# Even and odd tokens apart in a token tile: dilated attention within a parity, probabilities transposed in place, values in one visit

## The chip, the core and the metric

One core of a Trainium2 chip runs the program. The metric is the device time of one execution in microseconds (us), shown as the median of several runs. TensorE is called PE below (PEld is its weight load), VectorE DVE, ScalarE ACT, and SP is the engine whose queue issues most of the loads.

## The reference, cut to what matters

Three blocks in a row work on 256 tokens of width 1024: a feed-forward block, a mixer (a gated linear recurrence beside sliding-window attention with 16 heads) and a second feed-forward block; then two equal layers, each with a short convolution branch, a latent attention with 8 heads (MLA) and a dilated attention, all gated and summed. Everything is fp32.

The dilated attention has 3 groups of 8 heads of width 64. Group 0 looks back over 128 tokens one by one; group 1 sees every 4th token up to 512 back, group 2 every 16th up to 2048 back. With 256 tokens the last two see every key of their own residue that isn't in the future.

```
DIL_PATTERNS = ((128, 1), (512, 4), (2048, 16))
s = q.k * scale - slope * dilation * j      # j steps back, 0 <= j <= window // dilation
o_g, lse_g = softmax over the keys of group g
o_c = sum over g of softmax(lse)_g * o_g    # one softmax over the keys of all three groups
```

So a query of group 1 or 2 only ever attends to keys whose distance is a multiple of 4 or 16: always an even one.

## The kernel before, in words

Tokens stand in two tiles of 128 (a tile is one set of partitions). Every large product is made in three matmuls, high times high, high times low, low times high (`mm3`, L222 to L226), and its weights are streamed: SP loads a piece into one of 4 buffers `raw`, ACT rounds it to `w` high (L207), DVE subtracts to `w` low (L208), into one of 8 buffers. These streams are the bulk of PE's work: `gu`, `dn` (feed-forward), `g`, `xg` (mixer), `dqk`, `bz`, `gp`, `po`, `cx`, `zb`, `o` (layers).

Attention is threaded into the streams. After every few matmuls a stream calls `tick`, which advances a modelled time and lets one of three lanes issue its next piece: `tp` (transposes of queries and keys), `S` (scores and softmax) and `T` (values). The order in which the pieces are issued is thus set by that modelled time; each engine then works in order.

A layer has four `DilPair`s (m = 0 to 3), each with two heads (j) of all three groups. For each pair:

- `chunk`/`evac` project queries, keys and values (`dqk`); values are copied from PSUM to `vd` by two ACT copies (L1221).
- `scores` (L1248) goes over the three groups. `score_pair` (L787) makes for each head a 128x128 product for the first token tile and a 128x256 one for the second; the head's 64 channels stand in its own 64 partitions. A custom DVE operation adds scaled distances (1e33 where a key is not seen) and takes the maximum (L1260); after the third group ACT takes the exponentials (L1268), DVE sums and scales them (L1269 to L1274).
- `values` (L1277) goes over the groups again: `prob_T` (L771) transposes three 128x128 blocks for each head into a PSUM bank, ACT copies them to a tile `pt` (L776), and `pv_pair` (L779) accumulates values times probabilities in `dyT`, each head in its own 64 output columns. So PE is visited three times for values. `gated` then multiplies by the gate.

The mixer's attention (`attn1`) and MLA use `heads` (L712), which has the same pieces for one group: 8 pairs of heads in the mixer and 4 in each layer; each pair is a score piece, two `prob_T` and a value piece `yT`.

At the start SP loads the first token tile in two halves (`load_x`, L274), then the gain `g`, the first weight piece and the second token tile; at the end `residual` (L1131) adds and stores each tile in two halves.

Of the kernel before, what the change touches and what calls it, by code (L numbers as in the profile page):

```python
# [14 lines left out]
ALU = mybir.AluOpType  # L15
# [12 lines left out]
MIXER_POOLS = (("l2", 13), ("s", 4), ("pt", 4), ("gth", 2), ("c1", 3))  # L28
LAYER_POOLS = (("dil", 9), ("s", 5), ("pt", 4), ("gth", 2), ("c1", 3))
# [18 lines left out]
def host_constants():  # L48

    f = np.float32  # L50
    pos = np.arange(S, dtype=f)

    def rope(half, inv):
        ang = pos[:, None] * inv[None, :]
# [8 lines left out]
    q = np.arange(P)[:, None]  # L63
    k = np.arange(S)[None, :]
    diff = P + q - k
    dist = []
    for window, dil in ((128, 1), (512, 4), (2048, 16)):
        ok = (diff >= 0) & (diff % dil == 0) & (diff // dil <= window // dil)
        dist.append(np.where(ok, diff.astype(f), f(1e33)))
    kk = k[:, :P]  # L70
# [4 lines left out]
    slopes = (f(2.0) ** (f(-8.0) * np.arange(1, 25, dtype=f) / f(24))).astype(f)  # L75
    qs = np.broadcast_to((f(-0.125) / slopes)[None, :], (P, 24))
    pack = np.concatenate([c2, s2] + dist + [mask2, qs, c1, s1, mask1], 1)
    return np.ascontiguousarray(pack.astype(f)), [float(x) for x in slopes]
# [3 lines left out]
CW = CONST.shape[1] - 512  # L82

# [13 lines left out]
class Kern:  # L97
# [176 lines left out]
    def load_x(self, t):  # L274
        for f in range(2):
            c = slice(f * 512, (f + 1) * 512)
            self.nc.sync.dma_start(out=self.h[t][:, c], in_=self.a["x"][0, t * P:(t + 1) * P, c])

    def params(self):
# [13 lines left out]
        self.dist = take(768).rearrange("p (g k) -> p g k", g=3)  # L293
# [275 lines left out]
    def mixer(self, xT):  # L569
# [142 lines left out]
    def heads(self, pairs, v, mask, scale, emit, deps, out, sinks=None):  # L712
# [39 lines left out]
        def values():  # L752
            for m in range(len(pairs)):
                while len(ready) <= m or self.now < ready[m][1]:
                    yield 0.0, 0.3
                s = ready[m][0]
                yp = self.bank("yp", "yT", (P, S))
                pts = []
                for j in range(2):
                    yield from self.room()  # L760
                    pts.append(self.prob_T([s[:, j, b * P:(b + 1) * P] for b in range(3)]))
                    yield 0.32, W_T
                self.live -= 1
                self.pv_pair(yp, v[m], pts, True, True)
                emit(m, yp)
                yield 1.1, 0.0
# [12 lines left out]
    def pv_pair(self, yp, v, pts, first, last):  # L779
        m = self.nc.tensor.matmul  # L780
        for b in range(2):
            c = slice(P * b, S)
            for j in range(2):
                m(yp[64 * j:64 * j + 64, c], lhsT=v[j][b], rhs=pts[j][:, 0:S] if b == 0 else pts[j][:, S:384],
                  start=first and b == 0, stop=last and b == 1)
# [9 lines left out]
    def lru(self, pp, xT, w, out):  # L795
# [19 lines left out]
        for j in range(2):  # L815
            f = f0 + j
            xpad = self.tl("c1", [P, S + 3], "xpad")
            nc.vector.memset(xpad[:, 0:3], 0.0)
            nc.scalar.copy(xpad[:, 3:], banks[j][:, 0])
            xc = self.t([P, S], "xc")  # L820
            nc.scalar.activation(xc, xpad[:, 0:S], AF.Identity, scale=self.conv_w[:, 0, f:f + 1], bias=self.conv_b[:, f:f + 1])
            for k in range(1, 4):
                stt(xc, in0=xpad[:, k:k + S], scalar=self.conv_w[:, k, f:f + 1], in1=xc, op0=ALU.mult, op1=ALU.add)
            xcs.append(xc)
        for j in range(2):
            gb = banks[j][:, 1]
            u = self.t([P, S], "gu2")
            nc.scalar.activation(u, gb, AF.Square)
            stt(u, in0=u, scalar=1.0 / 0.044715, in1=gb, op0=ALU.add, op1=ALU.mult)
            nc.scalar.activation(u, u, AF.Tanh, scale=0.7978845608028654 * 0.044715)  # L830
            stt(GG[:, j], in0=u, scalar=1.0, in1=gb, op0=ALU.add, op1=ALU.mult)
# [269 lines left out]
    def conv_branch(self, l, xT, w):  # L1101
# [5 lines left out]
        for pp in range(2):  # L1107
# [3 lines left out]
            for j in range(2):  # L1111
                f = 2 * pp + j
                upad = self.tl("c1", [P, S + 2], "upad")
                nc.vector.memset(upad[:, 0:2], 0.0)
                tmp = self.t([P, S], "ac")
                nc.scalar.copy(tmp, b1[j][:, 0])
                tt(upad[:, 2:], tmp, b1[j][:, 1], op=ALU.mult)
                nc.scalar.activation(cv[:, j], upad[:, 0:S], AF.Identity, scale=cw[:, 0, f:f + 1], bias=cb[:, f:f + 1])
                for k in range(1, 3):
                    stt(cv[:, j], in0=upad[:, k:k + S], scalar=cw[:, k, f:f + 1], in1=cv[:, j], op0=ALU.mult, op1=ALU.add)  # L1120
            b2 = self.pairB(rows(xT), [col(3), col(0)], "zb")
            for j in range(2):
# [3 lines left out]
                tt(cv[:, j], cv[:, j], b2[j][:, 1], op=ALU.mult)  # L1126
                stt(cv[:, j], in0=cv[:, j], scalar=0.5, in1=sz, op0=ALU.mult, op1=ALU.mult)
                self.split(hi[:, f], lo[:, f], cv[:, j])
        return (hi, lo)

    def residual(self, t, accs, out=None):  # L1131
        nc = self.nc
        for f in range(2):
            c = slice(f * 512, (f + 1) * 512)
            nc.vector.tensor_tensor(self.h[t][:, c], accs[f], self.h[t][:, c], op=ALU.add)
            if out is not None:
                nc.sync.dma_start(out=out[t * P:(t + 1) * P, c], in_=self.h[t][:, c])
# [56 lines left out]
class DilPair:  # L1194
# [21 lines left out]
    def evac(self, which, ts, accs):  # L1216
        k, nc, m = self.k, self.k.nc, self.m
        if which == 2:
            self.dst[2] = k.tl("dil", [P, 2, 384], "vd")
            for t in ts:  # L1220
                nc.scalar.copy(self.dst[2][:, t], accs[t])  # L1221
# [3 lines left out]
        if which == 0 and self.gt is None:  # L1225

            self.gt = k.tl("pt", [P, 6, 64], "gt")
# [13 lines left out]
    def attend(self, sz, yc, out):  # L1241
        k, nc, m = self.k, self.k.nc, self.m
        ready = []
        qd, kd, vd = self.dst[0], self.dst[1], self.dst[2]
        sides = ((0, slice(0, P), slice(P, S)), (1, slice(P, 384), slice(0, S)))
        rows = [slice(64 * j, 64 * j + 64) for j in range(2)]

        def scores():  # L1248
            yield from k.after(*self.jobs)
            mx, nm, rs = (k.small([P, 2, 2], x) for x in ("dmx", "dnm", "drs"))  # L1250
            sm = k.small([P, 2, 2, 3], "dsm")
            ss = []
            for g in range(3):
# [3 lines left out]
                ps = k.score_pair([(qd[r, g], kd[r, g]) for r in rows])  # L1257
                for j in range(2):
                    for t, c, dc in sides:
                        nc.vector.tensor_tensor_reduce(  # L1260
                            s[:, j, c], in0=ps[j][:, c], in1=k.dist[:, g, dc], scale=-SLOPES[8 * g + 2 * m + j],
                            scalar=-3e38 if g == 0 else mx[:, j, t:t + 1], op0=ALU.add, op1=ALU.max, accum_out=mx[:, j, t:t + 1])
                yield 1.1, W_SC
            nc.vector.tensor_scalar(nm, mx, -1.0, None, op0=ALU.mult)
            for g, s in enumerate(ss):
                for j in range(2):
                    for t, c, _ in sides:
                        nc.scalar.activation(s[:, j, c], s[:, j, c], AF.Exp, bias=nm[:, j, t:t + 1], accum_out=sm[:, j, t, g:g + 1])  # L1268
            nc.vector.tensor_reduce(rs, sm, axis=mybir.AxisListType.X, op=ALU.add)  # L1269
            nc.vector.reciprocal(rs, rs)  # L1270
            for s in ss:
                for j in range(2):
                    for t, c, _ in sides:
# [3 lines left out]
        def values():  # L1277
            if not yc:
                yc.extend([k.b4([P, 4, S], "ych", F32R), k.b4([P, 4, S], "ycl", F32R)])
            while not ready or k.now < ready[0][1]:  # L1280
                yield 0.0, 0.3
            yp = k.bank("yp", "dyT", (P, S))
            for g, s in enumerate(ready[0][0]):
                pts = []
                for j in range(2):
                    yield from k.room()
                    pts.append(k.prob_T([s[:, j, b * P:(b + 1) * P] for b in range(3)]))
                    yield 0.32, W_T
                k.live -= 1
                k.pv_pair(yp, [[vd[:, b, (2 * g + j) * 64:(2 * g + j + 1) * 64] for b in range(2)] for j in range(2)], pts, g == 0, g == 2)  # L1290
                yield 1.1, 0.0
            k.gated(yc, sz, m, yp)
            yield 0.64, 0.0
# [36 lines left out]
```

## Time and profile before

| | |
|---|---|
| runs | 1349.64, 1346.84, 1347.28 us, median 1347.28 |
| the profiled execution | 1345.55 us, of which 1343.8 us are the span from first to last instruction |
| PE busy | 1313.7 us (98% of the span), 9434 matmuls |
| PE weight loads busy | 1215.6 us (90%) |
| DVE busy | 948.5 us (71%) |
| ACT busy | 784.5 us (58%) |
| DMA | 230.30 MB, mean 171 GB/s |

Busy times are unions of an engine's instructions. PE's are pipelined: two that follow each other overlap in the listing, so what one costs is read from start to start. A program matmul on fp32 data (scores, values) stands in the trace as two matmul records, each with its own weight load; one of `mm3` stands as one.

### The profile page before, as it was taken

What the parts mean: (1) busy time and instruction counts of PE and PEld (TensorE: products, weight loads), DVE (VectorE), ACT (ScalarE), POOL (GpSimd) and SP (SyncE); (2) the same over time, 40 slices, a digit from 0 to 9 for tenths busy, and PEclk for the clock granted to TensorE, in tenths of its full rate; (3) what the DMA queues carried; (4) which work ended last, traced back from release to release, by engine and by line L of the source; (5) the groups of instructions that cost most, each with busy time, mean ns of one, the idle gap of its engine ahead of it and who ended that gap; (6) DMA issues with size and microseconds to landing.
All of it is one profiled execution on the core that took longest, in us unless ns stands there. A gap on an engine that the chain in (4) does not pass through costs nothing.

```text
span 1343.8 us, 24690 instructions
## 1 busy us (share of the span) xinstructions
PE 1313.7 (98%) x9434; PEld 1215.6 (90%) x9434; DVE 948.5 (71%) x2178; ACT 784.5 (58%) x1468; POOL 3.0 (0%) x10
## 2 busy tenths in 40 slices
PE   6999999999999999999999999999999999999998
PEld 5899988989997899998998889999899988899997
DVE  6547667897868655568888676666788886765663
ACT  6444544788745544455667776554456667755451
POOL 0000000000000000000000000000000000000000
PEclk9999999999999999999999999999999999999999
DMA  7757764445565566673755454666656543546661
GB/s 255 226 166 234 224 219 142 139 146 135 169 213 179 176 197 191 205 231 98 212 142 131 126 173 126 180 186 194 179 157 186 142 128 104 173 145 187 193 195 52
DMA packets 234806, 230.30 MB, mean 171 GB/s; under 512 B 12336, under 2 KB 213184, under 8 KB 234688
## 3 DMA queue, kind: packets, MB, share of 16 engines
q1 hardware_dynamic: 232432, 227.05, 56.8%
q10 hardware_dynamic: 2256, 1.67, 0.5%
q8 instruction: 74, 1.21, 0.4%
q14 instruction: 44, 0.36, 0.1%
HBM read 227.64 MB, written 1.05 MB: 170 GB/s over the span
## 4 chain that ended last, share of the span: by engine, by line
PE 75%; DVE 11%; ACT 6%; DMA 5%; issue 2%; SPq 0%; ACTq 0%; DVEq 0%
PE gu L224 5%; PE gu L226 5%; PE gu L225 5%; PE gp L224 3%; DVE w L208 3%; PE gp L225 3%; PE gp L226 3%; PE dqk L224 3%; PE dqk L226 3%; PE dn L226 3%; PE dn L225 3%; PE dqk L225 3%; PE dn L224 3%; DMA raw<-in_w_in_dram 3%; PE po L224 2%
## 5 line engine op out<-in xcount | busy, mean ns | idle before, releaser
L208 DVE TENSOR_TENSOR w<-raw,w 128x1024 fp32r<-128x1024 f32 (+1 forms) x437 | 501.8, 1156 | 222.3 <-ACT w L207 218.5
L207 ACT CAST w<-raw 128x1024 fp32r<-128x1024 f32 (+1 forms) x437 | 433.3, 999 | 334.4 <-PE gu L226 51.1
L224 PE MATMUL gu<-xh,w 128*128 128x256 f32 x576 | 159.6, 277 | 0.0
L226 PE MATMUL gu<-xh,w 128*128 128x256 f32 x576 | 159.2, 276 | 0.0
L225 PE MATMUL gu<-xl,w 128*128 128x256 f32 x576 | 159.1, 276 | 0.0
L224 PE MATMUL dqk<-w,xh 128*128 128x384 f32 x384 | 136.5, 355 | 0.0
L225 PE MATMUL dqk<-w,xh 128*128 128x384 f32 x384 | 129.5, 337 | 0.0
L226 PE MATMUL dqk<-w,xl 128*128 128x384 f32 x384 | 129.2, 336 | 0.0
L225 PEld LDWEIGHTS gu<-xl,w 128*128 128x128 f32 x576 | 108.2, 188 | 0.6
L224 PEld LDWEIGHTS gu<-xh,w 128*128 128x128 f32 x576 | 108.1, 188 | 0.6
L224 PE MATMUL gp<-xh,w 128*128 128x256 f32 x384 | 108.3, 282 | 0.0
L226 PEld LDWEIGHTS gu<-xh,w 128*128 128x128 f32 x576 | 108.2, 188 | 0.0
L226 PE MATMUL gp<-xh,w 128*128 128x256 f32 x384 | 106.4, 277 | 0.0
L225 PE MATMUL gp<-xl,w 128*128 128x256 f32 x384 | 106.2, 277 | 0.0
L224 PEld LDWEIGHTS dqk<-w,xh 128*128 128x128 f32 x384 | 72.2, 188 | 6.2 <-issue 6.0
L224 PEld LDWEIGHTS gp<-xh,w 128*128 128x128 f32 x384 | 72.1, 188 | 2.7 <-issue 2.7
L225 PEld LDWEIGHTS dqk<-w,xh 128*128 128x128 f32 x384 | 72.4, 189 | 0.2
L226 PEld LDWEIGHTS gp<-xh,w 128*128 128x128 f32 x384 | 72.2, 188 | 0.0
L226 PEld LDWEIGHTS dqk<-w,xl 128*128 128x128 f32 x384 | 72.2, 188 | 0.0
L225 PEld LDWEIGHTS gp<-xl,w 128*128 128x128 f32 x384 | 72.2, 188 | 0.0
L226 PE MATMUL dn<-w,aT 128*128 128x512 f32 x176 | 69.1, 393 | 0.0
L225 PE MATMUL dn<-w,aT 128*128 128x512 f32 x176 | 68.9, 391 | 0.0
(378 smaller groups left out, 3242.6 us busy)
## 6 DMA issues: line engine op xcount, KB each, us to landing
raw<-in_w_in_dram SPq DMA_DIRECT2D x140, 512.0 KB
raw<-in_ffn_w_gu_dram SPq DMA_DIRECT2D x88, 512.0 KB
raw<-in_w_in_dram SPq DMA_DIRECT2D x192, 192.0 KB
raw<-in_ffn_w_down_dram SPq DMA_DIRECT2D x44, 512.0 KB
raw<-in_w_o_dram SPq DMA_DIRECT2D x16, 512.0 KB
raw<-in_w_proj_attn_dram SPq DMA_DIRECT2D x16, 256.0 KB
raw<-in_w_proj_lru_dram SPq DMA_DIRECT2D x8, 512.0 KB
raw<-in_w_out_dram SPq DMA_DIRECT2D x8, 512.0 KB
```

The source lines that it names most:

```text
L207: nc.scalar.copy(hi, raw)
L208: nc.vector.tensor_tensor(lo, raw, hi, op=ALU.subtract)
L224: m(out, lhsT=ah, rhs=bh, start=first, stop=False)
L225: m(out, lhsT=ah, rhs=bl, start=False, stop=False)
L226: self.last = m(out, lhsT=al, rhs=bh, start=False, stop=last).ins
```

## The change

Inside each tile of 128 tokens the order becomes: the 64 even ones, then the 64 odd ones. Loads of x and stores of the output are split by parity (twice as many, half as large), tables of cosines, masks and distances are built in that order, and where the order in time matters (the convolutions and the recurrence) operations that are there anyway read or write through a view that puts the tokens back (`natural`, `by_parity`). One operation of the mixer (L831) becomes two halves.

Groups 1 and 2 then need only products within a parity: `score_parity` makes, for each group, head j and parity e, a 64x128 and a 64x64 product, written for both groups into one pair of PSUM banks as large as those of one group before. Softmax thus goes over two score tiles instead of three. Values for groups 1 and 2 are kept by parity (`vp`), with the first tile's values of both groups above each other, so that one product serves both groups there.

`prob_T` copies the transposed blocks back over the probabilities; the tiles `pt` are gone. In `values` all transposes come first, then all value products in one visit; `heads` takes two pairs of heads together.

```diff
-MIXER_POOLS = (("l2", 13), ("s", 4), ("pt", 4), ("gth", 2), ("c1", 3))
-LAYER_POOLS = (("dil", 9), ("s", 5), ("pt", 4), ("gth", 2), ("c1", 3))
+MIXER_POOLS = (("l2", 13), ("s", 5), ("gth", 2), ("c1", 3))
+LAYER_POOLS = (("dil", 9), ("s", 5), ("v0", 2), ("gt", 2), ("gth", 2), ("c1", 3))
...
+def natural(x):
+    return x.rearrange("p (t i e) -> p t e i", i=64, e=2)
+def by_parity(x):
+    return x.rearrange("p (t e i) -> p t e i", i=64, e=2)
...
     def load_x(self, t):
+        x = self.a["x"][0, t * P:(t + 1) * P].rearrange("(i e) c -> e i c", e=2)
         for f in range(2):
             c = slice(f * 512, (f + 1) * 512)
-            self.nc.sync.dma_start(out=self.h[t][:, c], in_=self.a["x"][0, t * P:(t + 1) * P, c])
+            for e in range(2):
+                self.nc.sync.dma_start(out=self.h[t][64 * e:64 * e + 64, c], in_=x[e, :, c])
...
-                        self.split(yl[c][0][:, q], yl[c][1][:, q], out[2 * c + i])
+                        flat = lambda z: z.rearrange("p f s -> p (f s)")
+                        self.split(by_parity(flat(yl[c][0][:, q])), by_parity(flat(yl[c][1][:, q])), natural(flat(out[2 * c + i])))
...
-    def prob_T(self, parts):
-        ps = self.bank("x", "pT", (P, 384))
-        for b, x in enumerate(parts):
-            self.nc.tensor.transpose(ps[:, b * P:(b + 1) * P], x, self.id)
-        pt = self.tl("pt", [P, 384], "pt")
-        self.nc.scalar.copy(pt, ps)
-        return pt
+    def prob_T(self, s):
+        for j in range(2):
+            yield from self.room()
+            ps = self.bank("x", "pT", (P, 384))
+            for b in range(3):
+                c = slice(b * P, (b + 1) * P)
+                self.nc.tensor.transpose(ps[:, c], s[:, j, c], self.id)
+            self.nc.scalar.copy(s[:, j], ps)
+            yield 0.32, W_T
...
     def evac(self, which, ts, accs):
         if which == 2:
-            self.dst[2] = k.tl("dil", [P, 2, 384], "vd")
-            for t in ts:
-                nc.scalar.copy(self.dst[2][:, t], accs[t])
+            v0, vp = k.tl("v0", [P, 2, P], "v0"), k.tl("dil", [P, 6, P], "vp")
+            self.dst[2] = v0, vp
+            g12 = [acc[:, P:384].rearrange("p (g c) -> p g c", g=2) for acc in accs]
+            for t in range(2):
+                for e in range(2):
+                    nc.scalar.copy(vp[64 * t:64 * t + 64, 2 * e:2 * e + 2], g12[t][64 * e:64 * e + 64])
+                nc.scalar.copy(v0[:, t], accs[t][:, 0:P])
+                if t == 0:
+                    for e in range(2):
+                        for g in range(2):
+                            nc.scalar.copy(vp[64 * g:64 * g + 64, 4 + e], g12[0][64 * e:64 * e + 64, g])
...
+        def score_parity():
+            ps = [k.bank("x", "sc", (P, 384)) for _ in range(2)]
+            for g in range(2):
+                for j, r in enumerate(rows):
+                    for e in range(2):
+                        tok = lambda t: slice(P * t + 64 * e, P * t + 64 * e + 64)
+                        o = ps[j][64 * e:64 * e + 64]
+                        nc.tensor.matmul(o[:, P + g * P:S + g * P], lhsT=qd[r, 1 + g, tok(1)],
+                                         rhs=kd[r, 1 + g].rearrange("p (t e i) -> p e t i", t=2, e=2)[:, e], start=True, stop=True)
...
+                        nc.tensor.matmul(o[:, g * 64:g * 64 + 64], lhsT=qd[r, 1 + g, tok(0)], rhs=kd[r, 1 + g, tok(0)], start=True, stop=True)
...
-            for g in range(3):
+            for i in range(2):
                 s = yield from k.s_tile(2)
...
-                ps = k.score_pair([(qd[r, g], kd[r, g]) for r in rows])
+                ps = score_parity() if i else k.score_pair([(qd[r, 0], kd[r, 0]) for r in rows])
...
+            s0, s1 = ready[0][0]
+            for s in (s0, s1):
+                yield from k.prob_T(s)
             yp = k.bank("yp", "dyT", (P, S))
...
+            k.pv_pair(yp, [[v0[:, b, hd[j]] for b in range(2)] for j in range(2)], s0, True, False)
+            for i, c in ((4, 0), (5, 64), (0, P), (2, P + 64), (1, S), (3, S + 64)):
+                o = c if c < S else c - P
                 for j in range(2):
...
+                    nc.tensor.matmul(yp[hd[j], o:o + 64], lhsT=vp[:, i, hd[j]], rhs=s1[:, j, c:c + 64], start=False, stop=i == 3)
```

How the order on PE moves is seen at the first value piece of a layer's dilated attention, inside the stream `dqk` of the next pair (sc are scores, dyT values, pT transposes of probabilities; a row is line, operation, what it writes and reads, output partitions x columns, how often). Before:

```order
L226 MATMUL dqk<-w,xl 128x384
L784 MATMUL dyT<-pt,vd 64x256 x2
L784 MATMUL dyT<-pt,vd 64x128 x2
L792 MATMUL sc<-qkd 128x128 x2
L792 MATMUL sc<-qkd 128x256 x2
L224 MATMUL dqk<-w,xh 128x384
```

With the change, on the same engine:

```order
L246 MATMUL dqk<-w,xl 128x384
L810 MATMUL dyT<-s,v_7183 64x256 x2
L810 MATMUL dyT<-s,v_7183 64x128 x2
L1352 MATMUL dyT<-s,vp 64x64 x12
L1299 MATMUL sc<-qkd 64x128 x4
L1305 MATMUL sc<-qkd 64x64 x4
L1299 MATMUL sc<-qkd 64x128 x4
L1305 MATMUL sc<-qkd 64x64 x4
L244 MATMUL dqk<-w,xh 128x384
```

What were three value pieces and two of three score pieces, spread over the stream, is now one value piece of 16 matmuls and one score piece of 16, which here follow each other. The copies of the values on ACT, in the first layer, were before:

```order
L207 CAST w<-raw 128x1024 x2
L1221 COPY vd<-dqk 128x384 x2
L207 CAST w<-raw 128x1024
```

and are now:

```order
L1257 COPY vp<-dqk 64x256 x2
L1258 COPY v_7183<-dqk 128x128
L1262 COPY vp<-dqk 64x128 x4
L1257 COPY vp<-dqk 64x256 x2
L1258 COPY v_7183<-dqk 128x128
```

Ten copies stand where two stood, ahead of the roundings of weights that follow on ACT.

## Rows read from the trace of the kernel before

**Rows 1.** The page's part 1: busy us, share, instructions of each engine.

```profile
PE 1313.7 (98%) x9434; PEld 1215.6 (90%) x9434; DVE 948.5 (71%) x2178; ACT 784.5 (58%) x1468; POOL 3.0 (0%) x10
```

**Rows 2.** Busy time by stretch: bounds, length, engines, granted clock, DMA share, GB/s.

```profile
600.00:780.00 180.00, 176.17 (x1123) 163.06 (x1122) 146.50 (x503) 119.38 (x276) 0.00 (x0) 1.00 0.49 133
780.00:970.00 190.00, 189.51 (x1558) 179.15 (x1557) 127.03 (x235) 106.90 (x192) 0.00 (x0) 1.00 0.62 181
```

**Rows 3.** Waits of PE: us in all, how many, the longest.

```profile
PE tp L391 <- DVE hn L380: 9.7, 1, 9.7
...
PE po L224 <- ACT ylh L214: 1.6, 1, 1.6
```

**Rows 4.** Timeline of PE, one value and one score piece: start, duration, instruction.

```profile
796.37 0.28 PE L226 MATMUL gp<-xh,w 128*128 128x256 f32 x1
796.58 0.87 PE L784 MATMUL dyT<-pt,vd 128*64 128x256 f32 x8
797.38 0.93 PE L792 MATMUL sc<-qkd 64*128 64x128 f32 x8
798.24 0.39 PE L224 MATMUL gp<-xh,w 128*128 128x256 f32 x1
798.46 0.28 PE L225 MATMUL gp<-xl,w 128*128 128x256 f32 x1
798.58 0.28 PE L226 MATMUL gp<-xh,w 128*128 128x256 f32 x1
798.69 0.49 PE L774 MATMUL pT<-ident,s 128*128 128x128 f32 x3
...
799.15 0.28 PE L225 MATMUL gp<-xl,w 128*128 128x256 f32 x1
```

**Rows 5.** Groups of PE's instructions by form (count; busy us, mean ns).

```profile
L774 PE MATMUL pT<-ident,s 128*128 128x128 f32 x240 | 39.4, 273 | 1.8 <-DVE mx L728 1.0 <-ACT qkd L1237 0.8
...
L784 PE MATMUL dyT<-pt,vd 128*64 128x256 f32 x96 | 15.7, 405 | 0.0
L792 PE MATMUL sc<-qkd 64*128 64x256 f32 x96 | 14.4, 377 | 0.0
...
L784 PE MATMUL yT<-pt,kv 128*64 128x256 f32 x32 | 5.9, 404 | 0.0
...
L784 PE MATMUL yT<-pt,vm 128*64 128x256 f32 x32 | 5.2, 404 | 0.0
```

**Rows 6.** Timeline of PE at 797.38 us, the window cut after two matmuls.

```profile
797.38 0.38 PE L792 MATMUL sc<-qkd 64*128 64x128 f32 x2
```

**Rows 7.** Chain of waits, a score piece of MLA (96 partitions deep).

```profile
701.97 1.31 PE sc L792 x8
```

**Rows 8.** Chain of waits, 736 to 800 us: start, us, what.

```profile
745.81 3.53 ACT s L1268 x16
...
750.14 2.75 DVE s L1274 x12
...
781.09 4.95 DMA raw<-in_w_in_dram
```

**Rows 9.** Groups of ACT's instructions by form.

```profile
L1268 ACT ACTIVATE s<-s,dnm 128x256 f32<-128x256 f32 x48 | 24.0, 500 | 0.0
...
L1221 ACT COPY vd<-dqk 128x384 f32<-128x384 f32 x16 | 7.2, 492 | 1.1 <-PE dqk L226 1.1
...
L214 ACT CAST ylh<-lGG 128x512 fp32r<-128x512 f32 x4 | 2.4, 624 | 2.8 <-DVE lGG L866 2.8
```

**Rows 10.** Timeline of the first 20 us: SP, DVE and ACT.

```profile
0.74 0.86 SPq L277 DMA_DIRECT2D h<-in_x_dram  x2
...
8.76 1.41 DVE L380 SCALAR_TENSOR_TENSOR hn<-h,rs,g 128x512 f32<-128x512 f32 x2 [2.46 <-DMA g<-in_ffn_pre_g_dram]
...
9.98 1.05 ACT L207 CAST w<-raw 128x1024 fp32r<-128x1024 f32 x1 [5.15 <-DMA raw<-in_ffn_w_gu_dram]
```

**Rows 11.** Timeline of the last 6 us: SP's stores.

```profile
1339.53 1.69 SPq L1137 DMA_DIRECT2D out_dram<-h  x2
```

More of the change, by code (lines that the diff above doesn't have):

```diff
@@ L51, in host_constants @@
     pos = np.arange(S, dtype=f)
+    r = np.arange(P)
+    within = 2 * (r % 64) + r // 64
+    order = np.concatenate([within, P + within])
     def rope(half, inv):
-        ang = pos[:, None] * inv[None, :]
+        ang = pos[order][:, None] * inv[None, :]
         c, s = np.cos(ang), np.sin(ang)
@@ L62, in host_constants @@
     c2, s2 = rope(16, theta ** (-np.arange(0, 32, 2, dtype=f) / f(32)))
-    q = np.arange(P)[:, None]
-    k = np.arange(S)[None, :]
+    slopes = (f(2.0) ** (f(-8.0) * np.arange(1, 25, dtype=f) / f(24))).astype(f)
+    q = within[:, None]
+    k = order[None, :]
     diff = P + q - k
[L66 to L70, printed above, removed]
+    dist0 = np.where((diff >= 0) & (diff <= 128), diff.astype(f), f(1e33))
+    half = 2 * (r % 64)[:, None]
+    first, second = [], []
+    for dil, unit in ((4, 1.0), (16, 2.0 ** (-8.0 / 3))):
+        for into, dd in ((first, half - 2 * np.arange(64)[None, :]), (second, P + half - 2 * np.arange(P)[None, :])):
+            into.append(np.where((dd >= 0) & (dd % dil == 0), (dd * unit).astype(f), f(1e33)))
+    kk = within[None, :]
     causal = np.where(kk <= q, f(0), f(-8e30))
@@ L292, in params @@
         self.sin2 = take(64).rearrange("p (t d) -> p t d", t=2)
-        self.dist = take(768).rearrange("p (g k) -> p g k", g=3)
+        self.dist0 = take(256)
+        self.dist12 = take(384)
         self.mask2 = take(256)
@@ L752, in values, with pv_pair @@
         def values():
[L753 to L766, printed above, removed]
+            for m0 in range(0, len(pairs), 2):
+                ms = (m0, m0 + 1)
+                for m in ms:
+                    while len(ready) <= m or self.now < ready[m][1]:
+                        yield 0.0, 0.3
+                    yield from self.prob_T(ready[m][0])
+                yp = self.bank("yp", "yT", (P, 2, S))
+                for m in ms:
+                    self.live -= 1
+                    self.pv_pair(yp[:, m - m0], v[m], ready[m][0], True, True)
+                for m in ms:
+                    emit(m, yp[:, m - m0])
+                yield 2.0, 0.0
         self.spawn("S", scores())
         out.append(self.spawn("T", values()))
-    def prob_T(self, parts):
-        ps = self.bank("x", "pT", (P, 384))
-        for b, x in enumerate(parts):
-            self.nc.tensor.transpose(ps[:, b * P:(b + 1) * P], x, self.id)
-        pt = self.tl("pt", [P, 384], "pt")
-        self.nc.scalar.copy(pt, ps)
-        return pt
-    def pv_pair(self, yp, v, pts, first, last):
+    def prob_T(self, s):
[7 more added lines that the diff above has]
+            yield 0.32, W_T
+    def pv_pair(self, yp, v, s, first, last):
         m = self.nc.tensor.matmul
@@ L1225, in evac @@
         if which == 0 and self.gt is None:
-            self.gt = k.tl("pt", [P, 6, 64], "gt")
+            self.gt = k.tl("gt", [P, 6, 64], "gt")
             for i in range(3):
@@ L1281, in values @@
                 yield 0.0, 0.3
+            s0, s1 = ready[0][0]
+            for s in (s0, s1):
+                yield from k.prob_T(s)
             yp = k.bank("yp", "dyT", (P, S))
-            for g, s in enumerate(ready[0][0]):
-                pts = []
+            hd = rows
+            k.pv_pair(yp, [[v0[:, b, hd[j]] for b in range(2)] for j in range(2)], s0, True, False)
+            for i, c in ((4, 0), (5, 64), (0, P), (2, P + 64), (1, S), (3, S + 64)):
+                o = c if c < S else c - P
                 for j in range(2):
[L1286 to L1291, printed above, removed]
+                    nc.tensor.matmul(yp[hd[j], o:o + 64], lhsT=vp[:, i, hd[j]], rhs=s1[:, j, c:c + 64], start=False, stop=i == 3)
+            k.live -= 2
             k.gated(yc, sz, m, yp)
-            yield 0.64, 0.0
+            yield 2.0, 0.0
         k.spawn("S", scores())
```

54 lines of the change are left out of this document (33 added, 21 removed).

## The prediction

> **What bounds the kernel now.** I read the page first: PE is busy for 1313.7 of 1343.8 us [rows 1]. Busy is not yet bound, so the second view is the busy time by stretch. [...] The third is PE's list of waits: the largest is the 9.7 us before the first transposes, at the start; the next that this change touches is 1.6 us in the mixer, for the rounded recurrence output `ylh` [rows 3]. So nearly every microsecond is a PE instruction behind another one, and what the change is worth is what PE's attention pieces cost from start to start, less the waits that come in their place.
>
> **What a piece costs now.** The timeline of PE shows one value and one score piece inside a stream of 256-column matmuls [rows 4]. The stream's matmuls start 0.115 us apart (a mean; single steps round to 0.11 or 0.12). The value piece starts at 796.58, the score piece at 797.38, the stream again at 798.24: 0.80 and 0.86 us. From the stream's matmul at 796.37 to its second one after the pieces, at 798.46, are 2.09 us; two steps would be 0.23, the pieces are 1.66, and 0.20 us are left: what leaving and entering the stream costs, once for a stay, however many pieces it holds. The three transposes start at 798.69; from 798.58 to 799.15 are 0.57 us instead of 0.23, so a `prob_T` costs 0.34.
>
> Inside a piece, each matmul is two records. A score piece has 8 [rows 4], 4 of 128 and 4 of 256 columns; its first two, one for each head, begin together, so that both are inside 0.38 us [rows 6]. A score piece of MLA, whose heads are 96 partitions deep, has the same 8 records and takes 1.31 us [rows 7]. [...]
>
> **The change, part by part.**
>
> *Transposes.* 240 records are 80 `prob_T` of three [rows 5]; the eight dilated pairs have 6 each, and now 4. 16 x 0.34 = **5.5 us** less.
>
> *Scores.* 96 records of 256 columns, four to a piece, are 24 pieces in the dilated attention [rows 5]. The two pieces for groups 1 and 2 (16 in all, 13.8 us) become one parity piece (8 in all). It has 32 records: 16 of 128 columns and 16 of 64, in four places of the array (two heads by two parities). What four at once cost no row shows. If all four run side by side, as two do now, the columns take 4 x 0.107 + 4 x 0.053 = 0.64 us, and with 0.16 for the ends (weights of 64 columns, as in a value piece) 0.80: 6.4 us, **7.4 us** less. If only two run at once it is 1.28 + 0.16 = 1.44: 2.3 us less. I take the first: a value piece has two streams that read the same partitions and a score piece two that lie in different ones, each pair side by side; the new piece only combines the two.
>
> *Values, dilated.* 96 records of 256 columns are 24 pieces [rows 5], 19.2 us. Now 8 of them: 0.64 us for group 0, then 24 records of 64 columns, two heads side by side, 12 x 0.053 = 0.64, and the ends 0.16 make 1.44; 11.5 us, **7.7 us** less.
>
> *Values, mixer and MLA.* 64 records of 256 columns are 16 pieces [rows 5], 12.8 us; two at a time they have the ends once: 8 x (1.28 + 0.16) = 11.5, **1.3 us** less.
>
> *Stays.* In the order of PE's instructions, scores and values make 63 stays before and 42 now (fewer value pieces, but also fewer that share a stay with scores): 21 x 0.20 = **4.2 us** less.
>
> Together 26.1 us less on PE.
>
> *Added at the start.* Two more loads lie on SP's queue ahead of the gain and the first weights, and each takes 0.43 us to issue (0.86 for two) [rows 10]; the first norm waits for the gain until 8.76 and the first rounding for its weights until 9.98 [rows 10], so 0.9 us go on the path. The second tile's two loads push the weights behind them by as much again: 0 to 0.9 more. At the end SP issues two stores more; two now take 1.69 us with their wait [rows 11], so 0.4 (0 to 0.9). I take 0.9 + 0.4.
>
> *Added on ACT and DVE.* Ten copies of values instead of two of 0.49 us [rows 9]: together at least as long as now and at most 4.9 us, in a block ahead of weight roundings. Up to eight finished weight pieces, each 24 matmuls of 0.115 us in a stream like this, cover it; without that cover it would be 4 us on 8 places. Against it ACT loses four exponentials in a pair (0.5 us for 256 columns) [rows 9] and two copies of transposes. The reordered reads and writes have no row; the nearest are the same operations in order, so between as now and twice as long. They are hidden except at `ylh`, where PE waits already [rows 3]: ACT's 0.62 us [rows 9] and a DVE subtraction of about that length, so 0 to 1.3; I take 0.4. Sum added: **1.7 us**.
>
> 26.1 - 1.7 = 24.4 less. The profiled execution has 1345.55 us; that gives 1321.2. The median of the runs stands 1.7 above it, which I keep: **1323 us**.
>
> [...]
>
> **The rivals.**
>
> *Two at a time.* The four places share something that two don't, and the parity piece costs 1.44: 8 x 0.64 = 5.1 us more, 1328. For it: no row shows four. Against: both kinds of pair work.
>
> *The gain is lost before the value stage.* From 746 to 786 us the chain of waits doesn't run on PE alone, but through 16 exponentials (3.53 us), 12 scalings (2.75 us) and a late load (4.95 us) [rows 8]. Where that chain ends last, a shorter PE piece buys nothing, and the load stays late. In the order of PE's instructions about a third of a layer's dilated pieces stand there; of some 12 us in a layer 4 would be lost, twice: 1331. Against: a third of just these exponentials and scalings goes too, 2.1 us of the 6.3 in these rows and as much for the next pair, about what the ten copies add.
>
> *Slower: records bound by their supply.* [...] The wide stream shows that a weight load and a matmul can come every 0.115 us [rows 4]; no row shows that a long run gets them faster. At that rate a parity piece and a dilated value piece take 32 x 0.115 = 3.7 us each, 59 for the sixteen against 17.9: 41 us more than in my sum, and the time would be 1364. The point from which this decides is 26.1 - 1.7 + 17.9 = 42.3 us over 512 records: above 0.083 us a record the change is slower. [...]
>
> *It doesn't do what it says.* The products may be issued in an order in which heads or parities can't stand side by side; but the order of PE's instructions has them by fours, so this falls under the first rival.
>
> **How the numbers follow.** My case has 0.62, two at a time 0.13, the lost gain 0.12, a price for short records 0.09 (most of it slower, some at the 1337 of the rule or at no change), and 0.04 are for mishaps such as a new wait of some us. The range reaches from 1315, where DVE and ACT relieved of a third of this softmax also shorten some of PE's waits and the start costs nothing, to 1337, which takes in the first two rivals with the upper bounds of what is added. A measurement of this kernel can tell about 0.2% from no change, 2.7 us. Faster 0.89, same 0.04, slower 0.07.
>
> **What would show it.** In the profile after: about 24 us less span, nearly all in the two layers; a parity piece of 0.8 us (1.4: two at a time; over 2: supply); a dilated value piece of 1.4; 64 `prob_T` of 0.34; the first transposes at 10.5 instead of 9.65. PE still busy for 98%. I would be wrong if PE's share fell while its pieces cost what I say (a chain elsewhere), or if the matmuls of 64 columns cost as much as those of 128.

## The result, and the profile after

The changed kernel takes 1334.68 us (median of four runs, 1331.09 to 1335.83) against 1347.11 us of the kernel before in the same session. The ratio is 0.9899, with a 95% interval from 0.9877 to 0.9921: 12.4 us faster, inside the range, and half of the 24 forecast. The profiled execution took 1335.83 us, 1334.0 of them span; that is 9.8 us less span than before. On these 9.8 the readings below are made.

The page of the changed kernel, part 1 and the granted clock in 40 slices:

```profile
PE 1294.1 (97%) x9578; PEld 1212.3 (91%) x9578; DVE 934.7 (70%) x2090; ACT 781.3 (59%) x1452; POOL 3.0 (0%) x10
...
PEclk9999999999989999999999999999999999999999
```

PE's busy time fell by 19.6 us against [rows 1] and its share of the span by a point: it now waits more. The `PEclk` line has an 8: PE did not get its full clock throughout.

**The pieces cost what was forecast.** PE's timeline of the changed kernel around one value visit and one parity piece (start, duration, instruction, count):

```profile
776.47 0.34 PE L246 MATMUL dqk<-w,xl 128*128 128x384 f32 x1
776.74 0.87 PE L810 MATMUL dyT<-s,v 128*64 128x256 f32 x8
777.44 0.87 PE L1352 MATMUL dyT<-s,vp 128*64 128x64 f32 x24
778.24 0.45 PE L1299 MATMUL sc<-qkd 64*64 64x128 f32 x8
778.51 0.29 PE L1305 MATMUL sc<-qkd 64*64 64x64 f32 x8
778.62 0.40 PE L1299 MATMUL sc<-qkd 64*64 64x128 f32 x8
778.84 0.29 PE L1305 MATMUL sc<-qkd 64*64 64x64 f32 x8
779.07 0.44 PE L244 MATMUL dqk<-w,xh 128*128 128x384 f32 x1
```

From start to start the value visit takes 1.50 us (forecast 1.44) and the parity piece 0.83 (forecast 0.80). PE's group of transposes is 192 records, 64 `prob_T` of three, against 240 in [rows 5].

**PE waits more.** The largest of PE's waits in the changed kernel (us in all, times, longest):

```profile
PE tp L414 <- DVE hn L403: 10.5, 2, 9.9
PE uq L244 <- ACT cT L234: 4.0, 2, 2.4
PE po L244 <- ACT ylh L234: 2.9, 1, 2.9
...
PE dT L516 <- DVE hn L1045: 2.3, 1, 2.3
PE dT L516 <- ACT w L227: 2.3, 1, 2.3
```

Against [rows 3], `tp` has 0.8 us more (in two waits, where it was one) and `po` 1.3 more; `uq` had 1.5 before, and the two `dT` rows are new, one in each layer (the second, at 1157 us, is put down to `w`, but the first half of `hn` ends there at the same time, some 0.6 us after its start at 1156.31). Over the whole list PE waits for 35.2 us instead of 26.3.

**And its clock falls, behind some of these waits and elsewhere.** Windows of the changed kernel, busy time (and count) of PE, PEld, DVE, ACT and POOL, then granted clock, DMA share and GB/s:

```profile
278.00:282.00 4.00, 3.21 (x21) 2.24 (x20) 4.00 (x17) 2.40 (x4) 0.00 (x0) 1.00 0.00 0
282.00:285.40 3.40, 3.40 (x18) 3.40 (x17) 3.40 (x12) 2.07 (x9) 0.00 (x0) 0.50 0.55 167
375.00:378.30 3.30, 0.52 (x5) 0.32 (x3) 3.30 (x5) 0.62 (x1) 0.00 (x0) 0.89 0.39 130
377.50:384.30 6.80, 5.91 (x27) 5.91 (x28) 2.26 (x4) 1.70 (x2) 0.00 (x0) 0.50 0.46 154
797.00:799.50 2.50, 0.24 (x4) 0.00 (x1) 2.40 (x8) 1.86 (x4) 0.00 (x0) 1.00 1.01 310
800.80:804.20 3.40, 3.40 (x23) 3.28 (x20) 1.05 (x3) 1.94 (x8) 0.00 (x0) 0.50 0.89 283
1004.50:1009.00 4.50, 2.74 (x17) 2.14 (x14) 4.27 (x12) 4.47 (x9) 0.00 (x0) 1.00 0.97 334
1009.00:1012.40 3.40, 3.26 (x10) 3.26 (x11) 2.87 (x13) 2.57 (x6) 0.00 (x0) 0.50 0.48 127
```

The rows go in pairs: a stretch in which PE does less than its stream would, then one at a granted clock of 0.50. What PE had waited for was 0.2 and 0.6 us between score pieces ahead of the first fall, 2.9 us for `ylh` around the second, 2.3 us ahead of the third, 1.6 and 0.3 us ahead of the fourth. Four such stretches make 17 us, in which at most 8.5 us of full-clock work is lost. In the profiled execution of before, the clock fell nowhere within the work (mean granted clock 1.000). The behaviour is not the same in each run: the waits of 2.4 us at 648 and 2.3 us at 1154 us had no fall behind them, and over the four runs the mean granted clock was 0.999 (1331.09 us), 0.996 (1334.65), 0.995 (1334.70) and 0.993 (1335.83, the profiled one).

**The new wait in a layer.** The value visit of the second pair was issued in two parts, with the transposes of the last pair's queries and keys between them. PE's timeline of the changed kernel there:

```profile
796.38 0.87 PE L810 MATMUL dyT<-s,v 128*64 128x256 f32 x6
799.54 0.52 PE L516 MATMUL dT<-ident,hn 128*128 128x128 f32 x3 [2.30 <-DVE hn L1045]
799.99 0.32 PE L810 MATMUL dyT<-s,v 128*64 128x128 f32 x1
```

What these transposes wait for is read from DVE's timeline of the same stretch:

```profile
789.61 0.16 DVE L1329 TENSOR_REDUCE drs<-dsm 128x4 f32<-128x8 f32 x1 [2.94 <-ACT s L1328]
...
790.02 1.94 DVE L1334 TENSOR_SCALAR s<-s,drs 128x128 f32<-128x128 f32 x8
791.87 1.01 DVE L1056 TENSOR_REDUCE hss<-sq 128x6 f32<-128x384 f32 x2
...
793.33 0.17 DVE L273 TENSOR_TENSOR rt<-rs 128x12 f32<-128x12 f32 x1
793.44 1.23 DVE L228 TENSOR_TENSOR w<-raw,w 128x1024 fp32r<-128x1024 f32 x1
794.58 0.16 DVE L274 TENSOR_TENSOR rt<-rt,rv 128x12 f32<-128x12 f32 x1
...
798.84 1.03 DVE L1045 TENSOR_TENSOR hn<-hn,rs 128x384 f32<-128x384 f32 x2
```

The norm of the last pair's queries and keys is a chain of small steps. Most take 0.17 us, but between them stand four weight subtractions of 1.22 us, so that it lasts from 791.87 to the first `hn` at 799.41. None of that got shorter, and it starts later than it did. ACT copies the pair's product out ahead of the norm. In the kernel before, it did so as PE delivered it (PE was done with the product at 781.2 us):

```profile
781.26 0.48 ACT L1026 COPY hn<-dqk 128x384 f32<-128x384 f32 x1
```

In the changed kernel PE was done at 785.0, but the copy stands behind the third pair's eight exponentials:

```profile
788.99 0.50 ACT L1328 ACTIVATE s<-s,dnm 128x256 f32<-128x256 f32 x1
...
789.84 0.85 ACT L1054 COPY hn<-dqk 128x384 f32<-128x384 f32 x2
```

DVE waits for the same exponentials for 2.94 us and makes their scalings ahead of the norm. The `hn` step at the end of the chain, at 798.84 now, was this in the kernel before:

```profile
792.52 1.01 DVE L1017 TENSOR_TENSOR hn<-hn,rs 128x384 f32<-128x384 f32 x2
```

That is 6.3 us earlier, while PE came to its transposes at 793.4, 3.8 us earlier than now, and the layer as a whole began 3.8 us earlier. So against the layer's start PE is not early here; the chain is late, by 2.5 us. The eight scalings take 1.94 us, where twelve took 2.75 [rows 8]: the relief that the second rival counted on is there, but scalings and exponentials now stand ahead of this norm.

**Where the 9.8 us come from.** The same matmul in both profiled executions, after minus before: +1.8 us at the end of the first feed-forward, +0.2 at the end of the mixer's gates, +3.8 behind the wait for `ylh` and its low clock, and so to the end of the second feed-forward; in the first layer +1.1 ahead of the split visit and +6.3 behind it, −3.1 at the layer's end; −10.6 at the end of the second layer's attention, and −9.8 in span. So the mixer and the layers gain by their shorter pieces, and give it back at the two kinds of places above, the new waits and the stretches at the low clock.

### The profile page after: what moved, and what is told of

It is laid out like the page before. It is cut to its first block, busy times and chain, and to the rows that moved or that the text cites. A ratio compares the mean times of both kernels' runs of the same rounds, so it can differ in the third digit from the quotient of the medians.

```text
span 1334.0 us, 24880 instructions
## 1 busy us (share of the span) xinstructions
PE 1294.1 (97%) x9578; PEld 1212.3 (91%) x9578; DVE 934.7 (70%) x2090; ACT 781.3 (59%) x1452; POOL 3.0 (0%) x10
## 4 chain that ended last, share of the span: by engine, by line
PE 73%; DVE 12%; ACT 7%; DMA 5%; issue 3%; SPq 0%; ACTq 0%; DVEq 0%
PE gu L244 5%; PE gu L245 5%; PE gu L246 5%; PE gp L244 3%; DVE w L228 3%; PE gp L245 3%; PE gp L246 3%; PE dn L246 3%; PE dn L245 3%; PE dn L244 3%; PE dqk L244 2%; PE dqk L246 2%; PE dqk L245 2%; DMA raw<-in_w_in_dram 2%; PE po L244 2%
## 5 line engine op out<-in xcount | busy, mean ns | idle before, releaser
L228 DVE TENSOR_TENSOR w<-raw,w 128x1024 fp32r<-128x1024 f32 (+1 forms) x437 | 502.0, 1157 | 238.4 <-ACT w L227 235.9
```

The source lines that it names most:

```text
L228: nc.vector.tensor_tensor(lo, raw, hi, op=ALU.subtract)
```

## The experiments

Each ran beside the kernel before on the same chip, whose median was 1348.34 us in the first session, 1347.33 in the second and 1351.14 in the third.

**1. The token order alone.** Into the kernel before went the order and the views it needs, and nothing of the attention:

```diff
+    within = 2 * (r % 64) + r // 64
+    order = np.concatenate([within, P + within])
...
+            for e in range(2):
+                self.nc.sync.dma_start(out=self.h[t][64 * e:64 * e + 64, c], in_=x[e, :, c])
...
-            nc.scalar.copy(xpad[:, 3:], banks[j][:, 0])
+            nc.scalar.copy(natural(xpad[:, 3:]), by_parity(banks[j][:, 0]))
```

> The kernel before with the new token order alone: split loads and stores, permuted tables, reads and writes through the reordering views; attention, transposes and value visits as before. Theory 1 (the pieces on PE shrank as summed, and what is missing went into longer waits of PE at a few places and into stretches at the lower granted clock behind them): the order itself costs only the start and the end, 1 to 3 us, so 1348 to 1350 us. Theory 2 (the work that the new order adds eats half of the gain): 1355 to 1360 us.

Measured: 1351.03 us (ten runs), 1.0020 of before, 1.0007 to 1.0033: 2.7 us more. The order costs a little more than the 1.7 forecast for all that is added, and not the 12 us that are missing. Its profile has the start's two waits at 10.4 us in all, and `ylh` at 1.6, as before.

**2. The transposes in place and one visit alone.** Three groups and the old order stay:

```diff
+            for s in ss:
+                yield from k.prob_T(s)
...
+            for g, s in enumerate(ss):
+                k.pv_pair(yp, [[vd[:, b, (2 * g + j) * 64:(2 * g + j + 1) * 64] for b in range(2)] for j in range(2)], s, g == 0, g == 2)
```

> The kernel before with transposes in place and values in one visit, all three groups as before, tokens in their old order. By the pieces' prices: eight value visits of 1.92 + 0.16 instead of 24 of 0.80 (2.6 us less), two pairs of heads in one (1.3 less), 46 stays instead of 63 (3.4 less): 7.3 us less, 1340 us if nothing waits longer. Theory 1: 1340 to 1344, with longer waits in PE's list for the difference. A rival, that the single visit itself is what makes PE wait: no gain, 1346 to 1348.

Measured: 1340.61 us (five runs), 0.9938 (0.9918 to 0.9959), 7.7 us less by the medians and 8.4 by the ratio. PE's timeline has the visit with three groups:

```profile
812.61 2.17 PE L786 MATMUL dyT<-s,vd 128*64 128x256 f32 x24
814.71 0.93 PE L794 MATMUL sc<-qkd 64*128 64x128 f32 x8
```

It is 2.10 us long from start to start, and one visit gives what stays and ends are worth. So a long visit as such brings no loss that shows. But the longer wait for `ylh` is here already, with the tokens in their old order, and the low clock with it (a wait, then a window with the columns above):

```profile
PE po L224 <- ACT ylh L214: 3.1, 1, 3.1
...
372.40:375.80 3.40, 2.93 (x13) 2.93 (x14) 1.51 (x2) 0.42 (x1) 0.00 (x0) 0.50 0.74 229
```

So that wait doesn't need the new token order.

**3. A longer wait in the mixer.** In the kernel before, two maxima of a tile with itself, which change nothing, were put behind the last step of the fourth recurrence, ahead of the rounding to `ylh`:

```diff
+            if pp == 3:
+                for _ in range(2):
+                    tt(GG, GG, GG, op=ALU.max)
```

> The kernel before with two more passes of DVE (each 0.7 us, the maximum of a tile with itself) at the end of the mixer's fourth recurrence, so that PE waits longer before the product with the recurrence output. Theory 1, part on the clock (a longer wait of PE at this place is followed by a stretch at the lower granted clock): PE waits 1.4 us longer, 3 us in all, and the matmuls behind it run for some us at 1.2 GHz, which costs 2 to 4 us more: 1350 to 1353 us. The rival, that the clock falls for another reason: 1348.5 us and a granted clock of 1.00 there.

Measured: 1350.28 us (ten runs), 1.0017 (0.9996 to 1.0038). A miss: PE's wait for `ylh` stayed at 1.4 us, since other matmuls of the stream were issued ahead of it. The run doesn't test what it was made for; it shows that the order of instructions can absorb a delay that is known when the order is made.

**4. The transposes of queries and keys due later.** `W_D` is the modelled time between the norm of a pair and the moment at which its transposes may be issued. In the changed kernel:

```diff
-W_Q, W_C, W_D0, W_D = (10., 12., 14., 10.)
+W_Q, W_C, W_D0, W_D = (10., 12., 14., 13.)
```

> The changed kernel with one number: the transposes of normalised queries and keys of the pairs 1 to 3 are due 3 us later (13 instead of 10), so that those of the last pair no longer stand inside its predecessor's value visit. Theory 1: PE's waits for them (2.3 us, twice) and the lower clock behind the first go, 4.6 us and up to 1.7 more: 1328 to 1331 us. The rival, that the chain on DVE ends last anyway and PE waits for it a little further on: 1334 to 1335 us.

Measured: 1324.46 us (four runs), 0.9819 (0.9794 to 0.9845): 10 us less than the changed kernel, more than any theory gave, and where the forecast lay. PE's timeline has the visit whole, and the transposes behind it without a wait:

```profile
792.08 0.87 PE L810 MATMUL dyT<-s,v 128*64 128x256 f32 x8
792.78 0.87 PE L1352 MATMUL dyT<-s,vp 128*64 128x64 f32 x24
...
795.08 0.49 PE L516 MATMUL dT<-ident,hn 128*128 128x128 f32 x3
```

The norm still stands behind the third pair's exponentials (ACT copies the product at 784.0 us, PE was done with it at 780.8), but no visit stops for it. Of PE's waits, the two rows of `dT` for `hn` and `w` are gone; `ylh` stays as long as it was and has the one stretch at the low clock that is left behind it (waits, then windows with the columns above):

```profile
PE tp L414 <- DVE hn L403: 9.9, 2, 9.4
PE po L244 <- ACT ylh L234: 2.9, 1, 2.9
...
PE uq L244 <- ACT cT L234: 2.2, 2, 1.3
...
375.20:377.50 2.30, 0.59 (x5) 0.59 (x6) 2.30 (x4) 0.66 (x1) 0.00 (x0) 1.00 0.32 111
377.50:380.90 3.40, 3.40 (x19) 3.40 (x18) 0.40 (x1) 0.00 (x1) 0.00 (x0) 0.50 0.76 233
```

Between the profiled executions lie 12.7 us of span: by milestones 4.3 at the first layer's split visit and 2.8 at the second's; 2.6 are in the mixer and before it, the start included, where the number changes nothing but the clock fell for less time; most of the rest is at `uq`. So some 7 us of the 12.7 belong to the edit by place. The fastest executions of the two kernels, with a mean clock of 0.999 and 1.000, took 1331.09 and 1322.39 us: 8.7 us that the clock has next to no part in.

**5. The same number in the kernel before**, as a control:

```diff
-W_Q, W_C, W_D0, W_D = (10., 12., 14., 10.)
+W_Q, W_C, W_D0, W_D = (10., 12., 14., 13.)
```

> The control for the later transposes: the kernel before, unchanged but for the same number (13 instead of 10). Theory 1 (the number removes waits that the change had brought, inside value visits that are long): nothing to remove here, 1345 to 1349 us. The rival, that the number is worth its 10 us in any kernel: 1337 us.

Measured: 1346.09 us (ten runs), 0.9994 (0.9983 to 1.0005). The number was worth nothing before: the wait that it removes came with the change.

**6. Work ahead of the recurrence.** On top of run 4, the mixer's second gate product of the recurrence (`L`) comes before the first product that needs its output (`q`) and not after it:

```diff
-M_ORDER = 'xaxAxlxpPqLQ'
+M_ORDER = 'xaxAxlxpPLqQ'
-MIXER_POOLS = (("l2", 13), ("s", 5), ("gth", 2), ("c1", 3))
+MIXER_POOLS = (("l2", 13), ("s", 4), ("gth", 4), ("c1", 3))
```

> The changed kernel with the later transposes, and in the mixer the gate stream L ahead of the first product with the recurrence output instead of behind it (two more gate tiles, one score tile less), so that this stream runs while DVE finishes the recurrence. Theory 1: PE's wait of 2.9 us for the rounded recurrence output goes, and with it the 3.4 us at 1.2 GHz behind it (1.7 us): 3 to 5 us less than with the later transposes alone, 1318 to 1321 us. The rival, that the wait appears behind the second product or at the output projection: 1323 us.

Measured: 1318.74 us (four runs), 0.9792 (0.9771 to 0.9813). The wait for `ylh` is off the list, and PE is full at the high clock through this part of the mixer (a window of this run, columns as above):

```profile
340.00:400.00 60.00, 60.00 (x523) 59.79 (x522) 50.36 (x70) 37.70 (x52) 0.00 (x0) 1.00 0.66 212
```

Against run 4 the ratio falls by 0.0027, 3.6 us, somewhat less than the 4.6 that the wait of 2.9 and 3.4 us at half clock make; the two intervals overlap, so the size of this step is not sure.

**7 and 8. A wait forced where there was none.** On top of run 4, in the second layer's convolution, PE makes four transposes of a tile that DVE copies from the stream's last product, so that the stream stands still until it is done; in run 8 three maxima of 512 columns, again of the tile with itself, lengthen the wait (in run 7 that loop is empty). The question is whether a stretch at a granted clock of 0.50 stands behind the forced wait, as stretches of 3.4 and 6.8 us stood at waits of 2.3 and 2.9 us in the changed kernel; I expected one, at a cost of about half its length.

```diff
+            if l == 1 and pp == 1:
+                late = self.t([P, 512], "late")
+                nc.vector.tensor_copy(late, b1[1].rearrange("p i s -> p (i s)"))
+                for _ in range(3):
+                    tt(late, late, late, op=ALU.max)
+                for _ in range(4):
+                    ps = self.bank("acc", "lateT", (P, P))
+                    nc.tensor.transpose(ps, late[:, 0:P], self.id)
+                    nc.vector.tensor_copy(late[:, 0:1], ps[:, 0:1])
```

> The changed kernel with the later transposes and one forced wait: in the second layer's convolution, where PE runs without a gap, four transposes of a tile that DVE copies from the stream's last product, into all four banks that the next stream needs. Computes the same output; it adds the copy, the transposes and the wait. [...] The rival, that the clock doesn't follow PE's waits: granted clock 1.00 around the wait.

> As the kernel with the forced wait, with three more passes of DVE over 512 columns ahead of the transposes, a wait of some 5 us. [...] The rival: granted clock 1.00 around it, and the wait alone is lost.

Measured: 1333.38 and 1341.45 us, one run each. In run 7 PE waits 2.5 us and 2.0 more between the transposes, and the granted clock is 0.50 for 3.4 us from 1227.0. Windows of run 8 (columns as above) show the full stream, the wait, and what stands behind it:

```profile
1215.00:1225.70 10.70, 10.70 (x95) 10.53 (x93) 7.64 (x12) 5.45 (x8) 0.00 (x0) 1.00 0.68 197
1225.70:1234.50 8.80, 1.64 (x6) 0.79 (x5) 6.01 (x13) 2.30 (x4) 0.00 (x0) 0.66 0.42 122
1234.50:1238.50 4.00, 4.00 (x20) 4.00 (x20) 0.16 (x1) 0.00 (x0) 0.00 (x0) 0.50 0.00 0
1238.50:1245.00 6.50, 6.50 (x59) 6.50 (x58) 2.45 (x2) 2.26 (x3) 0.00 (x0) 0.99 0.29 80
```

The engine, full at a granted clock of 1.00, waits, and goes on at 0.50 with 5 matmuls a microsecond (20 in 4.0 us) where it made 9 (95 in 10.7 us). By the milestones this place costs 10.9 us, some 8.8 the wait with its transposes and 2 the slow matmuls behind it: the forced wait costs about a quarter more than it lasts. Both executions also had the low clock at other places (run 8 at 283, 378 and 1007 us), so their totals say nothing finer.

**9. Fewer loads at the start.** On top of run 6, each tile is loaded by parity in two whole-row pieces and not four:

```diff
-        for f in range(2):
-            c = slice(f * 512, (f + 1) * 512)
-            for e in range(2):
-                self.nc.sync.dma_start(out=self.h[t][64 * e:64 * e + 64, c], in_=x[e, :, c])
+        for e in range(2):
+            self.nc.sync.dma_start(out=self.h[t][64 * e:64 * e + 64], in_=x[e])
```

> The changed kernel with the later transposes, the gate stream ahead of the recurrence product, and each token tile of x loaded in two whole-row halves by parity (two loads a tile, as many as before the change, instead of four). Theory 1: the two extra issues on SP at the start go, about 0.9 us, perhaps 1.8: 1316.5 to 1318 us. The rival, that the start waits for the gain and the weights whatever the loads are: 1318.7 us.

Measured: 1318.84 us (five runs), 0.9766 (0.9746 to 0.9785). SP is done with the first tile 1.3 us earlier, but its norm now waits for whole rows: the first wait is 11.2 us. No gain that can be told from run 6, whose interval overlaps.

**10. Values projected before MLA.** On top of run 9, the first pair's value projection (`v`) comes ahead of MLA's first product, whose input was late (`uq`):

```diff
-L_ORDER = 'v0mmma1b'
+L_ORDER = '0mmma1b'
...
+        dil[0].chunk(xT, 2)
```

> As the kernel before it, with the projection of the first pair's dilated values moved ahead of the first MLA product in each layer, so that its stream of 8 us stands between the compressed queries and the product that needs them transposed. Theory 1: PE's waits for that transposed tile (2.8 us in two layers, and a further 1 to 2 us behind them) go: 2 to 4 us less, 1313 to 1316 us. The rival, that MLA's keys and queries then come late and PE waits for them or for their scores: 1317 to 1320 us.

Measured: 1317.76 us (four runs), 0.9755 (0.9739 to 0.9770), beside run 9's 0.9766 in the same session: the same. The wait of `uq` is gone from the head of the list, but others take its place (PE's waits of this run):

```profile
PE pT L799 <- ACT qkd L1277: 2.2, 2, 1.4
PE bz L244 <- ACT vm L1111: 1.5, 2, 0.7
```

Runs 4, 6, 9 and 10 beat both kernels. Against the kernel before, run 10 takes 0.9755 of the time, where the change by itself takes 0.9899.

## Why the prediction was half right

**Removed: right.** Of the 26.1 us on PE the pieces gave about 25.4: eight value visits at 1.50 instead of 1.44 (0.5 us short; read from the six that are whole), eight parity pieces at 0.83 instead of 0.80 (0.2 short). A lone value visit of two pairs took 1.655 us with its 0.20 for the stay, where 1.64 was counted; a `prob_T` 0.34; PE's order has 42 stays, as counted. The terms from which these prices were added up, 0.107 and 0.053 us for records of 128 and 64 columns and 0.16 for the ends, with the 0.64 and 1.28 us made of them, no run shows as such. What the runs showed in their place: in the changed kernel fours of 128 columns follow each other after 0.11 us, fours of 64 after 0.055, which leaves 0.17 of the 0.83 for the ends; in the value visit group 0 takes 0.70 us (0.64 counted) and its 24 short records 0.80 (0.64 and 0.16 counted).

**The two rivals on PE fall.** Two at a time would have been 1.44 us a parity piece, supply 3.7 us; it is 0.83, with 32 records, 26 ns each, against 83 ns as the point that decides. No run shows a price for short records that would lead to the 1337 us among the chances: 32 of them took 0.83 us in the parity piece, and the 24 of a value visit 0.80. PE's timeline of the changed kernel, cut after 0.03 us in the parity piece at 778.24 and at 778.84, has four records each time:

```profile
778.24 0.34 PE L1299 MATMUL sc<-qkd 64*64 64x128 f32 x4
...
778.84 0.24 PE L1305 MATMUL sc<-qkd 64*64 64x64 f32 x4
```

One of the last four lasts 0.22 us, so all four begin within some 0.02 us. So the records go by fours, and the next four follow after 0.11 us at 128 columns and 0.055 at 64: four places work side by side, as the forecast took it.

**Added: the step that failed.** "Sum added: 1.7 us" had three terms, for waits that stood in the trace. The order itself, measured alone, is 2.7 us (run 1), near enough. What is missing is a term for waits that the new order of issue brings. A transpose was issued at a modelled moment that had been late enough; now it stood inside the long value visit and ahead of its input. This is the second rival in kind, a chain beside PE that a shorter piece doesn't shorten. I looked for it in the exponentials, the scalings and a late load as the trace had them; it was the norm of the last pair, which had come ahead of such exponentials and scalings and now stands behind them, with weight subtractions between its own small steps. In the mixer it was the recurrence ahead of `ylh`: there PE came with its gain (+1.8 to +0.2 us) and waited it away. That the order is made from a modelled time was known from the code, and the diff leaves `W_D` as it was, while all around it got shorter.

**The clock: not in the sum at all.** I took 1.00 from [rows 2] for granted. Run 6 shows what that left out, since its profiled execution has the high clock throughout, in a span of 1315.2 us:

```profile
PE 1285.4 (98%) x9578; PEld 1204.5 (92%) x9578; DVE 934.4 (71%) x2090; ACT 782.1 (59%) x1452; POOL 3.0 (0%) x10
```

Its 9578 matmuls are those of the changed kernel, where, in another order in the mixer, they keep PE busy for 8.7 us more, about the 8.5 that 17 us at the low level lose. PE's idle time, span less busy time, is 39.9 us in the changed kernel, 30.1 before and 29.8 in run 6: 9.8 more than before, of which the sum had 1.7, so 8.1 are unforeseen. Clock and waits together are 16.8 us, in about equal shares. The span missed its forecast by 14.6 (24.4 less 9.8); the pieces' 0.7 come on top, and 2.9 go off again, since PE's busy time fell in run 6 by 28.3 us where the pieces' prices give 25.4. Where these 2.9 come from is not shown. The four runs of the changed kernel agree with the shares: the one with the clock at 0.999 was 4.7 us faster than the one with 0.993, and at 1331.09 us still 8 above the forecast. Runs 4 and 6 show that both go together: without the split visit the forecast of 1323 is reached (1324.46), and without the wait for `ylh` it is passed. The frequencies in GHz that some expectations name are shown by no run; what the traces have is the granted share of the full clock, 1.00 and, in the stretches above, 0.50.

**Covered work stayed covered.** ACT makes 80 copies of values now, 24.4 us in all (3.05 a chunk), within the 4.9 a chunk given as upper bound, and no wait of PE names them. The writes of `ylh` through the view took 670 ns each, where those in order took 624 [rows 9]: the reordering as such costs little, nearer to the lower bound than to the twice as long that was allowed.

**What would show it.** The first transposes start at 9.86 us, 0.2 later, not at 10.5 (the 10.5 us of `tp` are two waits); the first rounding starts 0.7 later. The rest of the start's loss comes behind them: it is 1.8 us at the end of the first feed-forward, twice the 0.9 that I took and as much as my upper bound. "I would be wrong if PE's share fell while its pieces cost what I say (a chain elsewhere)": that is what the page shows, 97% with pieces of 0.83 and 1.50.

What stays open: how much of the loss in one wait is the clock when the fall happens, why it follows one wait of 2.3 us and not another of 2.3 or one of 2.4 in the same execution, why it falls at 282 us where PE had waited for only 0.8 us in all, and what in the order of issue put the exponentials ahead of the last pair's norm.

## What to carry to other kernels

Price PE's pieces from start to start, then ask of each piece behind them what it waits for and whether *that* got shorter too: a cut on the bounding engine only counts up to the next input that comes from elsewhere. Where an order is made from modelled costs and due times, a change in the pieces makes the old due times wrong; one number went with 10 us here, some 7 of them at the places that it changes, and was worth nothing in the kernel it came from. For an input that is late, look at what stands ahead of its first step on its own engines. And a wait in a stream that is otherwise full can cost more than it lasts, because the matmuls behind it may run at the low clock: run 8 paid 10.9 us for 8.8, with matmuls at a granted clock of 0.50 behind the wait.

## What the runs showed of the hardware

- Four products of fp32 data, each 64 deep and 64 wide, ran side by side in the changed kernel: four records begin within some 0.02 us, and 32 take 0.83 us, while records of MLA, 96 deep, 8 in 1.31 [rows 7], ran one behind the other (PE's timeline of before from 701.81 us: 0.11 us apart at 128 columns, 0.22 at 256).
- PE's granted clock, 1.00 till then, fell to 0.50 for 3.4 or 6.8 us at or behind waits of 1.6 to 3.1 us, and once behind two of 0.2 and 0.6; at a forced wait of 6.2 us for 10.2 us, part of it within the wait. Other waits, of 2.3 and 2.4 us, had no such stretch behind them.
- A load of half as many partitions was no cheaper to issue. The first four loads of the changed kernel on SP's queue (start, duration, count), where two took 0.86 us [rows 10]:

```profile
0.73 2.49 SPq L299 DMA_DIRECT2D h<-in_x_dram  x4
```

  This is 0.62 us each against 0.43, though each moves half. The load of the gain that comes next, the same as before, took 0.59 us too, where it had taken 0.42, so the shape alone need not be the reason.
